# Dilated attention layer: TensorE order pinned, attention steps placed between dense products

## The chip, the cores and the metric

The kernel runs on one core of a Trainium2 chip. The metric is the time of one execution on the device in microseconds (us), the median of several runs.

## The reference

Two transformer blocks over 256 tokens of width 1024, fp32. The first has four layers, each an attention mixer and a SwiGLU FFN: differential attention (A), latent attention (B), dilated attention (C) and A again. The second block has two layers of a mixer with three branches and a convolutional FFN. The change lies in layer C, the third of the first block:

```python
C_GROUPS = ((128, 1), (512, 4), (2048, 16))   # window, dilation
C_HEADS = 16
C_HEAD_DIM = 64
...
    qkv = (h @ w_qkv).reshape(B, S, G, 3, C_HEADS, C_HEAD_DIM)
    q = apply_rope(qkv[:, :, :, 0], cos, sin) * (C_HEAD_DIM ** -0.5)
    k = apply_rope(qkv[:, :, :, 1], cos, sin)
    v = qkv[:, :, :, 2]
...
    wts = jax.nn.softmax(jnp.stack(lses, axis=0), axis=0)
    o = jnp.sum(wts[..., None].astype(v.dtype) * jnp.stack(outs, axis=0), axis=0)
    return o.reshape(B, S, C_HEADS * C_HEAD_DIM) @ w_o
```

Here `h` is the RMS-normalised input. Each of three groups looks at keys of its window and dilation; the groups are weighted by the softmax of their log-sums, so that one softmax over the scores of all three groups gives the same. Then come the residual and the FFN.

## The kernel before

All activations lie transposed in SBUF, 128 features by 256 tokens, eight such pieces for `x`. A dense product in fp32 is made of three matmuls (`mm3`, L259 to L261): both factors are split into a high and a low part, and high x high, high x low and low x high are added in PSUM. Weights come in tiles of 128x1024 by a DMA on the SyncE queue (`weights`, L271, tile `raw`, ring of `RAW` = 6); ScalarE writes the high part `whi` (through the helper `act`, L229) and VectorE the low part `wlo` (L276), both in rings of `SPL` = 6.

PSUM has three banks for dense products (`mm`), three for scores (`sc`) and two for transposes (`tp`).

Layer C (`dilated`) works in four quads of heads. For a quad, `qk_block` makes q and k of each of the three groups: `mmode` runs 48 products of 512 columns (two token halves, t = 0 and 1, in one `mm` bank each), ScalarE evicts them as `qtok` with the norm's factor `r`, VectorE rotates them, and they are transposed. For groups 1 and 2 four transposes per token half go into one `tp` bank, which ScalarE and VectorE copy out (`kz`, L613, the keys of two heads beside zeros). The first group needs more exact scores: `stacked` splits q and k again and transposes three groups of four (L570 q, L574 high k, L579 low k), each group into a `tp` bank that ScalarE (q, low k) or VectorE (high k, L575) empties. For every other quad `v_block` makes v for two quads in the same way.

The attention of a quad is eight steps (c, e, t: pair of heads, head, token half). A step is the scores (L860 for groups 1 and 2, L585 and L586 for the stacked ones, one `sc` bank), masking with the minimum on VectorE (L398, `aexp`), the exponential on ScalarE with its sum, reciprocal and normalising on VectorE (L869, L870), four transposes (L287) and their copy `aT` on VectorE (L875). After four steps 32 small products mix v (L882) into a `tp` bank, which is split into the output's pieces (`split`, L405). At the end `project` multiplies by w_co, 192 products of 256 columns, and adds to x (L888). The FFN follows with `rms`: squares on ScalarE, their sum on POOL (L438, `sqacc`), a matmul over ones (L444), power on POOL (L453).

The code is written quad after quad. A scheduler decides the order of the instructions on each engine before the kernel runs, by its own estimate of when each can start: it puts steps of one quad between dense products of the next as their inputs come ready.

Of the kernel before, what the change touches and what calls it, by code (L numbers as in the profile page):

```python
# [2 lines left out]

# [23 lines left out]
RAW, SPL, PIECES = 6, 6, 2  # L27
# [178 lines left out]
class Program:  # L206
    def __init__(self, tc, ins, out, at):
        self.tc, self.nc, self.ins, self.out, self.at = tc, tc.nc, ins, out, at
        self.ready = []
        with ExitStack() as ctx:  # L210
# [35 lines left out]
    def t2(self, name, shape=(512,)):  # L246
        return self.wk.tile([128, *shape], F32, name=name, tag="t2", bufs=7)
# [6 lines left out]

    def mm3(self, out, l, r, start, stop, **kw):
        lh, ll = l
        rh, rl = r
        mm = self.nc.tensor.matmul
# [27 lines left out]
    def transpose(self, out, in_):  # L286
        return self.nc.tensor.transpose(out, in_, self.ident)  # L287
# [21 lines left out]
    def mmode(self, aps, n, kb, xs):  # L309
        ps = [self.mm_bank()[:, :n] for _ in range(2)]  # L310
        for b, ap in enumerate(aps):
# [4 lines left out]
            for k, t in kt:  # L316
# [4 lines left out]
                         b == 0 and k == 0, b == len(aps) - 1 and k == kb - 1)  # L321
        return ps
# [118 lines left out]
    def rstd(self, acc, n, eps):  # L441
        ps = self.tp_bank()
        for t in range(2):
            self.nc.tensor.matmul(ps[:, t:t + 1], acc[:, t * 128:(t + 1) * 128], self.ones[:, 0:1],  # L444
                                  start=True, stop=True)
# [105 lines left out]
    def stacked(self, q, out, t):  # L551
# [17 lines left out]
        for h in range(4):  # L569
            nc.tensor.transpose(pt[:, h, :], sv[:, h, :], self.identr)  # L570
        a = self.act(qs[:, :, tk], pt)
        pt = self.tp_bank().bitcast(R).rearrange("p (c n) -> p c n", c=4)
        for h in range(4):
            nc.tensor.transpose(pt[:, h, :], k[:, h].rearrange("p a d -> p (a d)"), self.identr)  # L574
# [3 lines left out]
        for h in range(4):  # L578
            nc.tensor.transpose(pt[:, h, :], lo[:, h].rearrange("p a d -> p (a d)"), self.identr)  # L579
        self.act(kl[:, :, tk], pt)  # L580

    def stacked_scores(self, ps, qk, h, tk, start=True):

        qs, kd, kl = qk
        self.nc.tensor.matmul(ps, qs[:, h, tk], kd[:, h, :], start=start, stop=False)  # L585
        return self.nc.tensor.matmul(ps, qs[:, h, tk], kl[:, h, :], start=False, stop=True)  # L586

    def qk_block(self, w, xs, rms, tab, kz=None, scale=0.125):


        ps = self.mmode([w[0], w[1]], 512, 4, xs)
        r = rms()
# [3 lines left out]
        r8 = rms.r8  # L596
        stacked = kz is None
        out = [self.rslot(), self.rslot(), self.rslot()] if stacked else self.slot()[:, :2, :]
        for t in range(2):
            q = self.t2("qtok")  # L600
            self.act(q[:, :256], ps[t][:, :256], scale=r8[:, t:t + 1])
# [3 lines left out]
            if stacked:  # L605
                self.stacked(q, out, t)
                continue
            pt = self.tp_bank().rearrange("p (c n) -> p c n", c=4)
            for c in range(4):
                self.transpose(pt[:, c, :], q[:, c * 128:(c + 1) * 128])  # L610
            tk = slice(t * 128, t * 128 + 128)
            self.act(kz[0:64, 0, :, tk], pt[0:64, 2:4, :])
            self.nc.vector.tensor_copy(kz[64:128, 1, :, tk], pt[64:128, 2:4, :])  # L613
            self.act(out[:, :, tk], pt[:, 0:2, :])
        return out if stacked else (out, kz)
# [213 lines left out]
    def dilated(self, l, own):  # L829
# [18 lines left out]
        for hq in range(4):  # L848

            qk = [self.qk_block(wqk[g, hq], xs, r, "ropeC", kz[hq % 2][g], -0.125) for g in range(3)]  # L850
            if hq % 2 == 0:
                v = [self.v_block([wv[g, hq], wv[g, hq + 1]], xs, r) for g in range(3)]
            for c in range(2):
                es = {}
                for e in range(2):
                    for t in range(2):
                        tk = slice(t * 128, t * 128 + 128)
                        ps = self.sc_bank()
                        for g in (1, 2):
                            nc.tensor.matmul(ps[:, 128 * g + 128:128 * g + 256], qk[g][0][:, c, tk],  # L860
                                             qk[g][1][:, e, c, tk], start=True, stop=True)
                        self.stacked_scores(ps[:, :256], qk[0], 2 * c + e, tk)
                        mx = self.wk.tile([128, 1], F32, name="cmax", bufs=3)
                        ex = self.t2("aexp")
                        self.masked(ex, ps, self.maskC[:, t * 512:(t + 1) * 512], mx)
                        sm = self.wk.tile([128, 1], F32, name="csum", bufs=3)
                        self.act(ex, ex, AF.Exp, scale=-1.0, bias=mx, accum=sm)
                        rc = self.wk.tile([128, 1], F32, name="crec", bufs=3)
                        nc.vector.reciprocal(rc, sm)  # L869
                        nc.vector.tensor_scalar(ex, ex, rc, None, op0=OP.mult)  # L870
                        pt = self.tp_bank().rearrange("p (c n) -> p c n", c=4)
                        for kc in range(4):
                            self.transpose(pt[:, kc, :], ex[:, kc * 128:(kc + 1) * 128])
                        es[e, t] = self.t2("aT", (4, 128))
                        nc.vector.tensor_copy(es[e, t], pt)  # L875
# [601 lines left out]
```

## Time and profile before

| | us |
|---|---|
| median of 3 runs | 2367.68 (2367.56 to 2369.26) |
| the profiled execution | 2368.34 |
| its span | 2366.6 |
| PE busy | 2238.3 (95%) |
| VectorE (DVE) busy | 1699.8 (72%) |
| ScalarE (ACT) busy | 1297.7 (55%) |
| POOL busy | 425.3 (18%) |
| mean granted PE clock | 0.973 |

The span is the profiled execution's time between its first and its last instruction. PE, the matmul engine, bounds it; an instruction of another engine matters where PE waits for its result. The clock is the share of full speed (2.4 GHz) that PE was granted; at 0.50 (1.2 GHz) a matmul takes twice as long. Layer C reaches from 634.5 to 974.8 us.

### The profile page before, as it was taken

What the parts mean: (1) busy time and instruction counts of PE and PEld (TensorE: products, weight loads), DVE (VectorE), ACT (ScalarE), POOL (GpSimd) and SP (SyncE); (2) the same over time, 40 slices, a digit from 0 to 9 for tenths busy, and PEclk for the clock granted to TensorE, in tenths of its full rate; (3) what the DMA queues carried; (4) which work ended last, traced back from release to release, by engine and by line L of the source; (5) the groups of instructions that cost most, each with busy time, mean ns of one, the idle gap of its engine ahead of it and who ended that gap; (6) DMA issues with size and microseconds to landing.
All of it is one profiled execution on the core that took longest, in us unless ns stands there. A gap on an engine that the chain in (4) does not pass through costs nothing. (4 is left out here: it accounts for less than half of the span.)

```text
span 2366.6 us, 42382 instructions
## 1 busy us (share of the span) xinstructions
PE 2238.3 (95%) x16438; PEld 2087.9 (88%) x16438; DVE 1699.8 (72%) x2984; ACT 1297.7 (55%) x2352; POOL 425.3 (18%) x345
## 2 busy tenths in 40 slices
PE   8999999999998898899999999988989999798998
PEld 6899997999977787899988999877989998698998
DVE  6776656766556656766677767896798689858875
ACT  7764465544554444544587545543457564345763
POOL 1010012200100000100102002264352034434211
PEclk9999999999999999999999999998989999898999
DMA  6355553455653243355633656433435554243543
GB/s 241 125 165 184 157 161 107 142 185 157 196 181 104 97 160 99 131 186 156 210 126 108 217 158 196 148 123 102 157 131 194 162 178 156 98 135 133 188 155 104
DMA packets 111417, 361.76 MB, mean 153 GB/s; under 512 B 12400, under 2 KB 15600, under 8 KB 111216
## 3 DMA queue, kind: packets, MB, share of 16 engines
q1 hardware_dynamic: 108816, 355.45, 45.9%
q10 hardware_dynamic: 2256, 3.34, 0.4%
q8 instruction: 129, 2.11, 0.4%
q14 instruction: 72, 0.59, 0.1%
q0 software_dynamic: 144, 0.26, 0.1%
HBM read 358.22 MB, written 1.05 MB: 152 GB/s over the span
## 5 line engine op out<-in xcount | busy, mean ns | idle before, releaser
L229 ACT ACTIVATE whi<-raw 128x1024 fp32r<-128x1024 f32 (+2 forms) x744 | 722.2, 976 | 588.6 <-PE mm L260 295.0
L276 DVE TENSOR_TENSOR wlo<-raw,whi 128x1024 fp32r<-128x1024 f32 (+4 forms) x686 | 774.2, 1133 | 320.2 <-ACT whi L229 319.1
L259 PE MATMUL mm<-xh,whi 128*128 128x256 f32 x2496 | 712.7, 286 | 6.0 <-DVE early L1124 5.8
L260 PE MATMUL mm<-xl,whi 128*128 128x256 f32 x2496 | 712.0, 285 | 4.5 <-DVE xl L232 4.3
L261 PE MATMUL mm<-xh,wlo 128*128 128x256 f32 x2496 | 711.2, 285 | 2.6 <-DVE wlo L276 2.6
L259 PEld LDWEIGHTS mm<-xh,whi 128*128 128x128 f32 x2496 | 479.4, 192 | 8.8 <-issue 7.0
L260 PEld LDWEIGHTS mm<-xl,whi 128*128 128x128 f32 x2496 | 479.1, 192 | 6.9 <-DVE xl L232 5.7
L261 PEld LDWEIGHTS mm<-xh,wlo 128*128 128x128 f32 x2496 | 478.5, 192 | 4.0 <-DVE wlo L276 3.2
L259 PE MATMUL mm<-s,whi 128*128 128x256 f32 x1504 | 428.1, 286 | 7.4 <-DVE s L232 5.1
L260 PE MATMUL mm<-s,whi 128*128 128x256 f32 x1504 | 426.1, 284 | 0.0
L261 PE MATMUL mm<-s,wlo 128*128 128x256 f32 x1504 | 425.6, 284 | 0.0
L259 PEld LDWEIGHTS mm<-s,whi 128*128 128x128 f32 x1504 | 287.5, 192 | 12.7 <-DVE s L232 4.6
L260 PEld LDWEIGHTS mm<-s,whi 128*128 128x128 f32 x1504 | 288.1, 192 | 1.2 <-issue 0.8
L261 PEld LDWEIGHTS mm<-s,wlo 128*128 128x128 f32 x1504 | 288.2, 192 | 0.1
L259 PE MATMUL mm<-whi,xh 128*128 128x512 f32 (+3 forms) x608 | 240.0, 396 | 10.4 <-ACT whi L229 8.6
L260 PE MATMUL mm<-wlo,xh 128*128 128x512 f32 (+3 forms) x608 | 238.7, 393 | 0.9 <-DVE wlo L276 0.8
L261 PE MATMUL mm<-whi,xl 128*128 128x512 f32 (+3 forms) x608 | 238.0, 392 | 0.0
L276 POOL TENSOR_TENSOR wlo<-raw,whi 128x1024 fp32r<-128x1024 f32 x58 | 142.2, 2461 | 150.6 <-ACT whi L229 150.3
L438 POOL TENSOR_TENSOR sqacc<-sqacc,sq 128x256 f32<-128x256 f32 x56 | 59.5, 1063 | 584.0 <-ACT sq L229 581.3
L259 PEld LDWEIGHTS mm<-whi,xh 128*128 128x128 f32 x608 | 115.1, 189 | 32.7 <-ACT whi L229 8.6
L260 PEld LDWEIGHTS mm<-wlo,xh 128*128 128x128 f32 x608 | 115.2, 190 | 21.4 <-DVE wlo L276 2.0
L261 PEld LDWEIGHTS mm<-whi,xl 128*128 128x128 f32 x608 | 115.1, 189 | 20.5
(328 smaller groups left out, 2863.6 us busy)
## 6 DMA issues: line engine op xcount, KB each, us to landing
raw<-w_gu SPq DMA_DIRECT2D x176, 512.0 KB, 4.5
raw<-w_up SPq DMA_DIRECT2D x88, 512.0 KB, 4.2
raw<-w_zs SPq DMA_DIRECT2D x60, 512.0 KB, 3.9
raw<-w_out SPq DMA_DIRECT2D x64, 384.0 KB, 3.1
raw<-w_cqk SPq DMA_DIRECT2D x48, 512.0 KB, 4.3
raw<-w_out SPq DMA_DIRECT2D x64, 320.0 KB, 3.1
raw<-w_aqk SPq DMA_DIRECT2D x32, 512.0 KB, 4.4
raw<-w_cv SPq DMA_DIRECT2D x24, 512.0 KB, 3.9
```

The source lines that it names most:

```text
L229: return self.nc.scalar.activation(out, in_, func, bias=bias, scale=scale, **kw)
L259: mm(out, lh, rh, start=start, stop=False, **kw)
L260: mm(out, lh, rl, start=False, stop=False, **kw)
L261: return mm(out, ll, rh, start=False, stop=stop, **kw)
L276: e.tensor_sub(lo, raw, hi.bitcast(F32))
L438: self.nc.gpsimd.tensor_add(acc, acc, sq)
```

## The change

In layer C every matmul and transpose on PE is kept in the order in which the code issues it (`keep_in_program_order`), and the code issues it in a new order. `mmode` counts modelled time after each `mm3` (`tick`), and a queue (`later`) calls steps when their modelled time has come; `drain` empties the queue, up to a condition, without dense products.

- v of a quad pair comes before q and k, and a quad's groups in the order 1, 2, 0.
- The transposes of q and k, the scores, the turn (transposes of the exponentials) and the mixing products are steps in that queue, each with a delay behind what feeds it: 4.2 and 5.8 for the two token halves of groups 1 and 2, 5.5 and 7.9 for the stacked ones, 4.5 from scores to turn, 2.2 from turn to mixing.
- Mixing is done for each token half apart (16 products, into an `sc` bank); the splits of its result become 16 of half the size.
- The copy `aT` moves from VectorE to ScalarE (32).
- The eight steps of the last quad are issued between 132 of the 192 output products; the other 60 are not pinned. The additions to x follow each pair of pieces, and the last pair uses an `sc` bank.
- `RAW` is 5 and not 6; the ring `t2` (qtok, aexp, aT) has 9 buffers and not 7.

The number of matmuls stays the same. Of the diff, the functions that decide the order (in `qk_block` the part behind the product became a generator, `qk_tokens`; the body of `score` is that of before):

```diff
-RAW, SPL, PIECES = 6, 6, 2
+RAW, SPL, PIECES = 5, 6, 2
+US = {128: 0.11, 256: 0.12, 512: 0.235}
...
-        return self.wk.tile([128, *shape], F32, name=name, tag="t2", bufs=7)
+        return self.wk.tile([128, *shape], F32, name=name, tag="t2", bufs=9)
...
+    def matmul(self, *a, **kw):
+        i = self.nc.tensor.matmul(*a, **kw)
+        if self.woven:
+            self.tc.keep_in_program_order(i)
+        return i
+
+    def later(self, delay, step):
+        self.serial += 1
+        heappush(self.queue, (self.now + delay, self.serial, step))
+
+    def tick(self, us):
+        self.now += us
+        if not self.inside:
+            self.inside = True
+            while self.queue and self.queue[0][0] <= self.now:
+                heappop(self.queue)[2]()
+            self.inside = False
+
+    def drain(self, done=lambda: False):
+        while self.queue and not done():
+            self.now = max(self.now, self.queue[0][0])
+            self.tick(0.0)
...
-    def transpose(self, out, in_):
-        return self.nc.tensor.transpose(out, in_, self.ident)
+    def transpose(self, out, in_, ident=None):
+        i = self.nc.tensor.transpose(out, in_, self.ident if ident is None else ident)
+        if self.woven:
+            self.tc.keep_in_program_order(i)
+        return i
...
                 self.mm3(ps[t], (xh[:, tk], xl[:, tk]), w(k, 0, n),
                          b == 0 and k == 0, b == len(aps) - 1 and k == kb - 1)
+                if self.woven:
+                    self.tick(3 * US[n])
...
+        self.woven = True
+        v, done = {}, [0]
+        def values(hq):
+            for g in range(3):
+                v[hq // 2, g] = self.v_block([wv[g, hq], wv[g, hq + 1]], xs, r)
+        def queries(hq):
+            q12 = self.slot()
+            qk = {}
+            for g in (1, 2, 0):
+                ps = self.mmode([wqk[g, hq][0], wqk[g, hq][1]], 512, 4, xs)
+                toks = list(self.qk_tokens(ps, r, "ropeC", -0.125))
+                if g:
+                    qk[g] = q12[:, 2 * g - 2:2 * g, :], kz[hq % 2][g]
+                    for t in range(2):
+                        self.later(4.2 + 1.6 * t, lambda t=t, q=toks[t], o=qk[g]: feature(q, o, t))
+                else:
+                    qk[0] = [self.rslot(), self.rslot(), self.rslot()]
+                    for t in range(2):
+                        self.later(5.5 + 2.4 * t, lambda t=t, q=toks[t]: (self.stacked(q, qk[0], t), self.tick(0.9)))
+            return qk
+        def feature(q, out, t):
+            qT, kT = out
+            tk = slice(t * 128, t * 128 + 128)
+            pt = self.tp_bank().rearrange("p (c n) -> p c n", c=4)
+            for c in range(4):
+                self.transpose(pt[:, c, :], q[:, c * 128:(c + 1) * 128])
+            self.act(kT[0:64, 0, :, tk], pt[0:64, 2:4, :])
+            nc.vector.tensor_copy(kT[64:128, 1, :, tk], pt[64:128, 2:4, :])
+            self.act(qT[:, :, tk], pt[:, 0:2, :])
+            self.tick(0.44)
+        def score(hq, qk, c, t, e, es):
+            tk = slice(t * 128, t * 128 + 128)
...
+            self.tick(0.7)
+            self.later(4.5, lambda: turn(hq, c, t, e, ex, es))
+        def turn(hq, c, t, e, ex, es):
+            pt = self.tp_bank().rearrange("p (c n) -> p c n", c=4)
+            for kc in range(4):
+                self.transpose(pt[:, kc, :], ex[:, kc * 128:(kc + 1) * 128])
+            es[e] = self.t2("aT", (4, 128))
+            self.act(es[e], pt)
+            self.tick(0.44)
+            if e:
+                self.later(2.2, lambda: mix(hq, c, t, es))
+        def mix(hq, c, t, es):
+            if (hq // 2, 2) not in v:
+                return self.later(1.0, lambda: mix(hq, c, t, es))
+            po = self.sc_bank()[:, :128]
+            for kc in range(4):
+                g, tv = (0, kc) if kc < 2 else (kc - 1, t)
+                for e in range(2):
+                    h = hq % 2 * 256 + (2 * c + e) * 64
+                    self.matmul(po[64 * e:64 * e + 64, :], v[hq // 2, g][:, tv, h:h + 64],
+                                es[e][:, kc, :], start=kc == 0, stop=kc == 3)
+            oh, ol = os_[hq * 2 + c]
+            tk = slice(t * 128, t * 128 + 128)
+            self.split(oh[:, tk], ol[:, tk], po, 1.0)
+            done[0] += 1
+            self.tick(1.3)
+        def attention(hq, qk, delay, pace):
             for c in range(2):
                 for t in range(2):
+                    es = {}
+                    for e in range(2):
+                        self.later(delay, lambda c=c, t=t, e=e, es=es: score(hq, qk, c, t, e, es))
+                        delay += pace
+        values(0)
+        qk = queries(0)
+        attention(0, qk, 11.0, 5.4)
+        qk = queries(1)
+        attention(1, qk, 11.0, 5.0)
+        qk = queries(2)
+        self.drain(lambda: done[0] == 8)
+        attention(2, qk, 26.0, 5.4)
+        values(2)
+        qk = queries(3)
+        self.drain(lambda: done[0] == 12)
+        attention(3, qk, 10.5, 1.9)
+        last = lambda j, k, f: self.mm3(ps[j][:, f, :], wt[j](k, f * 128), os_[k], k == 0 and f == 0,
+                                        k == 7 and f == 1, skip_group_check=True)
+        ps, wt = {}, {}
+        for j in range(4):
+            wt[j] = self.weights(self.ins["w_co"][j], 256)
+            ps[j] = (self.mm_bank() if j < 3 else self.sc_bank()).rearrange("p (f n) -> p f n", f=2)
+            for k in range(6 if j < 3 else 4):
+                for f in range(2):
+                    last(j, k, f)
+                    self.tick(3 * US[256])
+        self.drain()
+        self.woven = False
+        for j in range(4):
+            for k in range(6 if j < 3 else 4, 8):
+                for f in range(2):
+                    last(j, k, f)
+            for f in range(2):
+                k = 2 * j + f
+                xv = perm(self.x[k])
+                nc.vector.tensor_add(xv, xv, flat(ps[j][:, f, :]))
```

How this moves instructions is shown at three places. The first is PE at the start of layer C: `sqacc` is the sum of squares, `mm_7739` and `mm_7740` (before), `mm_7671` and `mm_7672` (after) are banks of the product blocks being started. Before:

```order
L444 MATMUL tp_7661<-ones_80,sqacc_7638 128x1 [waits Pool_49]
...
L259 MATMUL mm_7739<-whi_7743,xh_76 128x512 [waits Activation_49]
L260 MATMUL mm_7739<-wlo_7744,xh_76 128x512 [waits DVE_49]
L261 MATMUL mm_7739<-whi_7743,xl_77 128x512
...
L261 MATMUL mm_7739<-whi_7779,xl_77 128x512
L259 MATMUL mm_7740<-whi_7743,xh_76 128x512 [waits PE_49,Activation_49]
```

After:

```order
L261 MATMUL tp_7662<-ones_80,sqacc_7639 128x1 [waits Pool_49]
...
L261 MATMUL mm_7671<-whi_7675,xh_76 128x512 [waits Activation_49]
L261 MATMUL mm_7671<-wlo_7676,xh_76 128x512 [waits DVE_49]
L261 MATMUL mm_7671<-whi_7675,xl_77 128x512
L261 MATMUL mm_7672<-whi_7675,xh_76 128x512 [waits Activation_49]
```

Before, fifteen products for one token half stand behind the matmul over ones ahead of the first for the other half; after, three do, and the fourth waits for ScalarE.

The second is PE at the stacked transposes of a quad (`qsplit`, `ksplit`, `klow` are the split parts of q and k). Before, both token halves:

```order
L570 MATMUL tp_8474<-identr_78,qsplit_8467 128x128 [waits DVE_49,PE_49]
L574 MATMUL tp_8480<-identr_78,ksplit_8468 128x128 [waits PE_49,Activation_49]
L260 MATMUL mm_8526<-wlo_8536,xh_76 128x512
...
L579 MATMUL tp_8486<-identr_78,klow_8469 128x128 [waits DVE_49,Activation_49]
L570 MATMUL tp_8507<-identr_78,qsplit_8500 128x128 [waits DVE_49]
L260 MATMUL mm_8526<-wlo_8566,xh_76 128x512
...
L574 MATMUL tp_8513<-identr_78,ksplit_8501 128x128 [waits Activation_49]
L579 MATMUL tp_8519<-identr_78,klow_8502 128x128 [waits DVE_49,Activation_49]
```

After, one token half (the first of each four transposes is shown, here and above):

```order
L261 MATMUL mm_8677<-whi_8686,xl_77 128x512
L315 MATMUL tp_8728<-identr_78,qsplit_8721 128x128 [waits DVE_49,PE_49]
L315 MATMUL tp_8734<-identr_78,ksplit_8722 128x128 [waits Activation_49]
L315 MATMUL tp_8740<-identr_78,klow_8723 128x128 [waits DVE_49,Activation_49]
L261 MATMUL mm_8676<-whi_8748,xh_76 128x512
```

Before, dense products lie between eight, eight and eight; after, each half's twelve follow one another.

The third is PE at the end of the last quad (`pk0` is the identity, `aexp` the exponentials, `mm_10416` and `mm_10204` output products). Before:

```order
L261 MATMUL mm_10416<-s4_7561,wlo_10413 128x256
L287 MATMUL tp_10232<-pk0_70,aexp_10225 128x128 [waits DVE_49,PE_49]
L287 MATMUL tp_10232<-pk0_70,aexp_10225 128x128 x3
L287 MATMUL tp_10252<-pk0_70,aexp_10245 128x128 [waits DVE_49,PE_49]
L287 MATMUL tp_10252<-pk0_70,aexp_10245 128x128 x3
L882 MATMUL tp_10259<-aT_10197,s4_9368 64x128 [waits PE_49]
```

After, one step of several:

```order
L261 MATMUL mm_10204<-s4_7561,wlo_10201 128x256
L315 MATMUL tp_10274<-pk0_70,aexp_10214 128x128 [waits DVE_49,PE_49]
L315 MATMUL tp_10274<-pk0_70,aexp_10214 128x128 x3
L261 MATMUL sc_10281<-kz10_7527,s4_9587 128x128 [waits PE_49]
...
L261 MATMUL mm_10204<-s4_7561,whi_10200 128x256
...
L315 MATMUL tp_10300<-pk0_70,aexp_10236 128x128 [waits DVE_49]
L315 MATMUL tp_10300<-pk0_70,aexp_10236 128x128 x3
```

Before, the last two turns follow one another with the mixing products behind them; after, a turn, the scores of a later step and six output products alternate.

## Rows read from the trace of the kernel before

**Rows 1.** The page: busy time per engine; granted PE clock in 40 slices (tenths).

```profile
PE 2238.3 (95%) x16438; PEld 2087.9 (88%) x16438; DVE 1699.8 (72%) x2984; ACT 1297.7 (55%) x2352; POOL 425.3 (18%) x345
...
PEclk9999999999999999999999999998989999898999
```

**Rows 2.** Waits of PE, 634.5 to 981.3: us in total, times, longest.

```profile
PE tp L287 <- DVE aexp L870: 23.5, 8, 3.1
PE tp L287 <- DVE qtok L390: 2.2, 8, 0.4
...
PE mm L259 <- ACT qtok L229: 0.9, 1, 0.9
...
PE mm L259 <- ACT s L229: 0.5, 1, 0.5
```

**Rows 3.** Timeline of PE, end of the first quad: start, us, instruction, idle before.

```profile
740.67 1.09 PE L287 MATMUL tp<-pk,aexp 128*128 128x128 f32 x4 [2.87 <-DVE aexp L870]
744.86 1.09 PE L287 MATMUL tp<-pk,aexp 128*128 128x128 f32 x4 [3.11 <-DVE aexp L870]
```

**Rows 4.** Timeline of DVE, the step whose transposes start at 740.67.

```profile
738.21 0.68 DVE L398 CUSTOM_DVE_ANT_0 aexp<-sc,maskC 128x512 f32<-128x512 f32 x1
...
740.04 0.48 DVE L870 TENSOR_SCALAR aexp<-aexp,crec 128x512 f32<-128x512 f32 x1
```

**Rows 5.** Stretches: length, busy us of PE, PEld, DVE, ACT, POOL, clock, DMA.

```profile
634.50:974.80 340.30, 311.93 (x1799) 255.71 (x1798) 211.40 (x404) 173.24 (x303) 13.95 (x13) 0.95 0.37 123
...
740.18:750.42 10.24, 6.64 (x42) 5.54 (x43) 5.18 (x17) 3.66 (x10) 0.00 (x0) 0.50 0.01 2
805.04:811.87 6.83, 5.20 (x37) 4.50 (x38) 3.18 (x12) 3.26 (x9) 0.00 (x0) 0.50 0.00 0
897.20:907.44 10.24, 6.68 (x42) 5.54 (x43) 5.18 (x17) 3.70 (x10) 0.00 (x0) 0.50 0.00 0
958.64:965.47 6.83, 4.13 (x34) 3.83 (x36) 2.27 (x6) 0.81 (x2) 0.98 (x2) 0.50 0.01 2
371.54:378.37 6.83, 5.69 (x20) 5.39 (x21) 2.35 (x7) 3.26 (x7) 1.54 (x1) 0.50 0.31 101
```

**Rows 6.** Groups by form, 634.5 to 974.8: busy us, mean ns, idle before.

```profile
L276 DVE TENSOR_TENSOR wlo<-raw,whi 128x1024 fp32r<-128x1024 f32 x80 | 100.1, 1255 | 61.9 <-ACT whi L229 61.5
L229 ACT ACTIVATE whi<-raw 128x1024 fp32r<-128x1024 f32 x81 | 85.2, 1057 | 53.1 <-PE mm L261 30.7 <-issue 16.8 <-ACT qtok L229 2.4
...
L875 DVE COPY aT<-tp 128x512 f32<-128x512 f32 x32 | 22.1, 690 | 25.0 <-PE tp L287 25.0
...
L229 ACT ACTIVATE s<-tp 128x512 fp32r<-128x512 f32 x16 | 9.0, 583 | 0.8 <-PE tp L579 0.6
...
L229 ACT ACTIVATE s<-mm,rstd 128x512 f32<-128x512 f32 x12 | 8.3, 688 | 12.0 <-PE mm L261 12.0
```

**Rows 7.** Timelines of PE and POOL at the start of the layer.

```profile
647.56 0.39 PE L260 MATMUL mm<-wlo,xh 128*128 128x512 f32 x1
647.80 0.39 PE L261 MATMUL mm<-whi,xl 128*128 128x512 f32 x1
...
649.10 1.63 POOL L453 TENSOR_TENSOR rstd<-ms,nhalf 128x2 f32<-128x2 f32 x1 [2.37 <-DVE ms L451]
```

**Rows 8.** Timeline of PE, a wait in the latent layer before.

```profile
372.68 0.63 PE L287 MATMUL tp<-pk,qtok 128*96 128x128 f32 x2 [3.06 <-DVE arec L808]
```

**Rows 9.** Timeline of PE, stacked transposes of the third quad.

```profile
813.57 0.51 PE L574 MATMUL tp<-identr,ksplit 128*128 128x128 f32 x4
813.91 0.46 PE L260 MATMUL mm<-wlo,xh 128*128 128x512 f32 x1
```

**Rows 10.** Timelines of POOL and PE behind the layer.

```profile
972.09 9.06 POOL L438 TENSOR_TENSOR sqacc<-sqacc,sq 128x256 f32<-128x256 f32 x7 [11.33 <-ACT sq L229]
...
981.32 0.50 PE L444 MATMUL tp<-ones,sqacc 128*128 128x1 f32 x4
```

**Rows 11.** The page: issues of DMA, KB each, us to landing.

```profile
raw<-w_cqk SPq DMA_DIRECT2D x48, 512.0 KB, 4.3
```

More of the change, by code (lines that the diff above doesn't have):

```diff
@@ L2 @@
 from contextlib import ExitStack
+from heapq import heappop, heappush
 import numpy as np
@@ L209, in __init__ @@
         self.ready = []
+        self.woven, self.now, self.queue, self.inside, self.serial = False, 0.0, [], False, 0
         with ExitStack() as ctx:
@@ L443, in rstd @@
         for t in range(2):
-            self.nc.tensor.matmul(ps[:, t:t + 1], acc[:, t * 128:(t + 1) * 128], self.ones[:, 0:1],
-                                  start=True, stop=True)
+            self.matmul(ps[:, t:t + 1], acc[:, t * 128:(t + 1) * 128], self.ones[:, 0:1],
+                        start=True, stop=True)
         return self.power(ps[:, 0:2], 1.0 / n, eps)
@@ L604, in qk_block @@
             self.rope(q.rearrange("p (h d) -> p h d", h=8)[:, :, :16], 8, 8, c2, s2)
[L605 to L615, printed above, removed]
+            yield q
     def v_block(self, w, xs, r):
@@ L847, in dilated @@
         os_ = self.split_slots(8)
[L848 to L852, printed above, removed]
-            for c in range(2):
[L854 to L875, printed above, removed]
-                po = self.tp_bank()[:, :256]
-                for t in range(2):
-                    for kc in range(4):
-                        g, tv = (0, kc) if kc < 2 else (kc - 1, t)
-                        for e in range(2):
-                            h = hq % 2 * 256 + (2 * c + e) * 64
-                            nc.tensor.matmul(po[64 * e:64 * e + 64, t * 128:t * 128 + 128], v[g][:, tv, h:h + 64],
-                                             es[e, t][:, kc, :], start=kc == 0, stop=kc == 3)
-                self.split(*os_[hq * 2 + c], po, 1.0)
@@ new lines, in feature @@
+        def feature(q, out, t):
[10 more added lines that the diff above has]
+            tk = slice(t * 128, t * 128 + 128)
+            ps = self.sc_bank()
+            for g in (1, 2):
+                self.matmul(ps[:, 128 * g + 128:128 * g + 256], qk[g][0][:, c, tk],
+                            qk[g][1][:, e, c, tk], start=True, stop=True)
+            self.stacked_scores(ps[:, :256], qk[0], 2 * c + e, tk)
+            mx = self.wk.tile([128, 1], F32, name="cmax", bufs=3)
+            ex = self.t2("aexp")
+            self.masked(ex, ps, self.maskC[:, t * 512:(t + 1) * 512], mx)
+            sm = self.wk.tile([128, 1], F32, name="csum", bufs=3)
+            self.act(ex, ex, AF.Exp, scale=-1.0, bias=mx, accum=sm)
+            rc = self.wk.tile([128, 1], F32, name="crec", bufs=3)
+            nc.vector.reciprocal(rc, sm)
+            nc.vector.tensor_scalar(ex, ex, rc, None, op0=OP.mult)
+            self.tick(0.7)
+            self.later(4.5, lambda: turn(hq, c, t, e, ex, es))
```

28 lines of the change are left out of this document (13 added, 15 removed).

## The prediction

> **What bounds the kernel now.** I read the page first. TensorE (PE) is busy for 95% of the span, so only its idle time and its slow stretches can be won; the strip of granted clock shows where it falls below full speed [rows 1]. The reader should see there that nothing general is wrong: a gain can only come out of particular holes. The waits of PE over the changed layer, from its first dense product at 634.5 to the first products of the FFN behind it, name those holes [rows 2]: eight waits for the normalised exponentials (`aexp`, DVE L870), 23.5 us in all, the longest 3.1, then eight short ones for the rotated q and k (2.2 us), and one at the start of the layer (0.9).
>
> The timeline says where the eight lie. The first quad of heads runs its eight attention steps between dense products of the next quad; its last two steps find no products left, and PE stands before their transposes for 2.87 and 3.11 us [rows 3]. The other three quads end alike, the last two waits of the eight being 2.43 and 3.11. The wait is a chain of one step: masking on DVE starts at 738.21, the transposes can start 2.46 us later, when DVE has normalised [rows 3, 4]. So 24 of 32 steps are covered by products and 8 are not.
>
> The table of stretches adds what the holes cost behind them [rows 5]. After each of the four ends the granted clock is 0.50, 1.2 instead of 2.4 GHz, for 10.24, 6.83, 10.24 and 6.83 us. PE was busy in these for 6.64 + 5.20 + 6.68 + 4.13 = 22.65 us, work of half that time at full clock: 11.3 us lost. **The four ends cost 23.5 + 0.5 + 11.3 = 35.3 us**, with 0.5 for the output products' wait for the last split [rows 2].
>
> **What the change removes.** Every matmul of the layer is pinned, and a queue counts modelled time (0.235 us for a 512-column product; 0.24 on the timeline [rows 7]) and puts scores, transposes and mixing products between dense ones, the steps of the last quad between output products. The dense products, scores, transposes and mixing products stay the same in number. So the four ends go, if the placing works: -35.3. The feature transposes are put 4.2 and 5.8 modelled us behind their product block, so the 2.2 us of waits for q and k go too [rows 2]. Floor: 2368.3 - 35.3 - 2.2 = 2330.8.
>
> **What it adds,** part by part.
>
> *Start of the layer.* Today the scheduler runs 15 products of one token half into the third bank while the norm is being computed, and then waits 0.9 us [rows 2]. Pinned, token halves alternate after every three products, and the fourth needs a bank that ScalarE (ACT) must first empty. The three end at about 648.2 (the third starts at 647.80, lasts 0.39). The emptying needs the power on POOL, done at 649.10 + 1.63 = 650.73 [rows 7], and one value eviction of 0.69 [rows 6]: 651.5 at the earliest. A wait of 3.4 in place of 0.9: +2.5. A wait of 3.06 earlier in the program [rows 8] lies beside a stretch of 6.83 us at clock 0.50 with 5.69 busy [rows 5], 2.85 lost; I take that as well: +2.9. Ends: 2 and 6. Sum here +5.4.
>
> *Stacked transposes* (q and split k of the first group, eight token halves). Today they come as eight, products, four or the like; two groups of four lie 0.34 us apart with no idle time [rows 9]. Now all twelve come in a row, on two PSUM banks, so the third four waits until the first bank is copied out: 0.46 us for the transposes, 0.58 for the copy on ACT [rows 6], less some 0.6 that PE needs to get there, leaves 0.4 to 0.5. When the ACT stands in a weight split (1.06 us, 81 of them in the layer, [rows 6]) it is up to 1.5. I take 0.8, nearer to the lower value since splits fill a quarter of ACT's time: 8 x 0.8 = +6.4; ends 0 and 10. The Trainium skill, "Perfetto Trace Analysis", section "Matmuls" (under "Optimizing Tensor Performance"), says that independent matmul groups should rotate through PSUM banks so that the emptying of one lies beside the next one's matmuls; twelve in a row on two banks go against it. By the rule this term exists, and by today's rows, which show no wait, it would be nothing and the sum 6.4 lower; the present order puts products between, so the trace agrees with the rule rather than with a zero.
>
> *Turns.* Each step's transposes come 4.5 modelled us after its score, in the traced costs 3.8 to 5.1 us of PE work, for a chain of 2.46 [rows 3, 4]. A weight split on each engine can stand ahead of a link: 1.06 on ACT, 1.26 on DVE [rows 6], 4.8 together, which a short cover misses by up to 1. Only some steps meet both: +2 over the steady steps; ends 0 and 6. The copy of transposed weights moves from DVE to ACT (32 x 0.69, [rows 6]): DVE falls from 211 us of the 340, ACT rises from 173 to 195, both far from full [rows 5]. No added cost of its own beyond the turns.
>
> *Two drains.* Where the queue is emptied between quads, the last transposes are followed at once by the mixing products that wait for the ACT copy: 0.69 and a semaphore, +1 (0 to 2). Among the output products the last steps lie beside products and beside each other's scores and mixing, with short holes behind the last copy and split: +1. At worst the last two waits come back whole, 6.
>
> *Start of the FFN.* Today POOL adds squares from 972.09 for 9.06 us (seven, 1.29 each) and the matmul over ones, behind the FFN's first 48 products, comes at 981.32, just after, without waiting [rows 10]. In the new order 36 output products stand between the end of the second x pair and the FFN, 24 behind the third; at 0.12 us the third pair is ready 2.9 us before it. ACT squares the second pair only behind the high parts of the third, some 2.5 us later, so six additions begin about 0.4 us before the FFN and end -0.4 + 6 x 1.29 = 7.3 us into it, while the matmul over ones is due behind 48 products of 0.12, after 5.7. +1.7, with the semaphores (0 to 4).
>
> *Ring of raw weights 6 to 5.* A 512 KB transfer takes 4.3 us to land [rows 11]; with both splits (1.06 + 1.26) a buffer is bound for 6.6 us, a fifth of it 1.3, and PE needs 12 x 0.235 = 2.8 us per tile. Nothing; hidden by dense work. Outside the layer the order changes by a few places in one attention layer and the convolutional FFN: 0, bounds -3 and +3.
>
> **The sum:** 2330.8 + 5.4 + 6.4 + 2 + 1 + 1 + 1.7 = 2348.3 against the profiled execution of 2368.3. The median of the runs, 2367.7, is 0.7 lower, so 2347.6; I say **2348**, -0.8%. A measurement of this kernel can tell about 0.2%, 4.7 us, from no change.
>
> **Rivals.**
>
> 1. *New waits all hidden* (start and FFN too, at their low ends): the floor plus 2 to 5, about **2334**. For it: 24 of today's steps run without a wait. Against: the bank limit at the start is forced by order. Chance 0.15.
>
> 2. *Slower: the pinned order waits at every turn.* PE may not run ahead any more; when `aexp` is late, dense products that are ready stand behind the transposes. The price is the mean wait per turn times 32. It cancels the gain at (2368.3 - 2346.3) / 32 = 0.7 us; a mean of 1.0, from a cover at 3.8 against a chain of 4.8 at every step, gives 2346.3 + 32 = **2378**, and more if the clock falls with it. For it: the copy now also sits on ACT ahead of the next exponential (0.69). Against: splits take 85 us of ACT and 100 of DVE in 340 [rows 5, 6], a quarter, so most links meet none. Chance 0.08.
>
> 3. *The last quad's end stays* because output products run out too early: 2.43 + 3.11 + 0.5 and half of 4.13 [rows 5] come back, 8.1, **2356**. Against: 132 products are woven in. Chance 0.06.
>
> 4. *Weights late* through the smaller ring, in bursts behind the reordered transfers: some 10 us, **2358**. Against: the arithmetic above. Chance 0.05.
>
> 5. *The change does nothing*, because the scheduler had reached the same order: **2367**. Against: the two orders differ at the places shown. Chance 0.03.
>
> **How the numbers follow.** The forecast has 0.61 and, by its terms' ends, reaches from 2330 to 2368; the other 0.02 is for causes that I don't see, slower. A range of **2336 to 2362** leaves out most of the first rival, the second and fifth, and the forecast's rim: about 2 in 10. Faster: forecast, rivals 1, 3 and 4 = 0.87; same: rival 5 and a little of 2 = 0.04; slower 0.09.
>
> **What would show it.** In the profile after, PE's waits for `aexp` should be under 6 us and none over 1.5, with no stretch at clock 0.50 in the four places; one wait of some 3.4 us after three products at the layer's start, with a low clock beside it; eight waits of 0.4 to 1.5 on the third four of the stacked transposes; a wait of 1 to 4 at the matmul over ones. The forecast is wrong if waits for `aexp` come back as 32 of about 1 us (rival 2), if whole waits of 2.5 to 3 us stand before the output products' end (3), or if waits for weight splits appear between dense products (4).

## The result and the profile after

The changed kernel takes 2340.99 us (median of 4 runs, 2339.84 to 2341.94), the one before 2367.99: ratio 0.9885, 95% interval 0.9868 to 0.9902. The forecast was 2348 in a range of 2336 to 2362; the gain came out at 27 us where 20 were forecast. The profiled execution of the changed kernel took 2339.84 us.

The page after, as in [rows 1]:

```profile
PE 2223.0 (95%) x16438; PEld 2078.4 (89%) x16438; DVE 1677.6 (72%) x2960; ACT 1316.7 (56%) x2392; POOL 422.4 (18%) x345
...
PEclk9999999999999999999999999988999999899999
```

PE is busy for 15 us less with the same number of instructions, mostly because fewer of them run at half clock: 100.6 us of its busy time lay in stretches at 0.50 before, 72.3 do now, and half of the difference is 14.2. Where the time went is best read between two points that both kernels have: the matmul over ones for the norm at the start of layer C, and that for the FFN behind it. Before, they start at 646.78 and 981.32 [rows 10], 334.54 us apart:

```profile
646.78 0.61 PE L444 MATMUL tp<-ones,sqacc 128*128 128x1 f32 x4 [0.96 <-POOL sqacc L438]
```

After, at 645.93 and 955.40, 309.47 apart: **25.1 of the 28.5 us of span lie in the layer.** (Below, "the layer" is this distance.) The waits of PE in it, to be read beside [rows 2]:

```profile
PE tp L315 <- ACT s L232: 4.6, 8, 1.0
PE mm L261 <- ACT s L232: 3.3, 1, 3.3
PE sc L261 <- ACT aT L232: 2.0, 1, 2.0
PE mm L261 <- ACT qtok L232: 1.1, 1, 1.1
PE mm L261 <- DVE xl L235: 1.0, 1, 1.0
PE tp L261 <- POOL sqacc L471: 1.0, 1, 1.0
PE tp L315 <- DVE s L608: 0.8, 1, 0.8
```

All products now have one line, L261, and all transposes L315. The reader should see that no wait for `aexp` and none for rotated q and k is left (23.5 and 2.2 us before), and that seven groups are listed now, 13.8 us in all. Two of these were there before: the wait at the matmul over ones (1.0), and that for the low part of x (`xl`, 1.0 now), which has this row in the list of before:

```profile
PE mm L260 <- DVE xl L232: 0.6, 1, 0.6
```

Of the four stretches at clock 0.50 none is left, and there is a new one at 648.44:

```profile
633.60:948.40 314.80, 301.66 (x1800) 251.01 (x1799) 190.43 (x377) 191.04 (x341) 12.44 (x11) 0.99 0.41 136
...
648.44:655.27 6.83, 4.62 (x11) 3.65 (x12) 1.02 (x2) 1.64 (x3) 1.44 (x1) 0.50 0.77 266
```

It lies beside the new wait at the start of the layer, seen on the timelines of PE, ACT and POOL:

```profile
645.93 0.61 PE L261 MATMUL tp<-ones,sqacc 128*128 128x1 f32 x4 [0.97 <-POOL sqacc L471]
...
646.95 0.40 PE L261 MATMUL mm<-whi,xl 128*128 128x512 f32 x1
650.65 0.80 PE L261 MATMUL mm<-whi,xh 128*128 128x512 f32 x1 [3.31 <-ACT s L232]
...
649.91 1.27 ACT L232 ACTIVATE s<-mm,rstd 128x512 f32<-128x512 f32 x2 [3.27 <-POOL rstd L486]
...
648.25 1.63 POOL L486 TENSOR_TENSOR rstd<-ms,nhalf 128x2 f32<-128x2 f32 x1 [2.37 <-DVE ms L484]
```

Three products, then PE waits 3.31 us for the first value eviction, which waits for the power on POOL. The stacked transposes show the other forecast wait, here one of the two longest of the eight (0.99 and 1.00), with ACT beside it:

```profile
715.46 0.50 PE L315 MATMUL tp<-identr,ksplit 128*128 128x128 f32 x4
716.96 0.54 PE L315 MATMUL tp<-identr,klow 128*128 128x128 f32 x4 [0.99 <-ACT s L232]
...
715.36 1.06 ACT L232 ACTIVATE whi<-raw 128x1024 fp32r<-128x1024 f32 x1 [1.20 <-PE mm L261]
716.33 0.58 ACT L232 ACTIVATE s<-tp 128x512 fp32r<-128x512 f32 x1
```

The low parts of k need the bank of q; its copy stands behind a weight split of 1.06 on ACT and starts only at 716.33. Where the queue is drained, the same happens to the copy of transposed exponentials:

```profile
819.85 0.88 PE L261 MATMUL sc<-aT,s 128*64 128x128 f32 x12 [2.05 <-ACT aT L232]
...
818.26 1.05 ACT L232 ACTIVATE whi<-raw 128x1024 fp32r<-128x1024 f32 x1
819.21 0.59 ACT L232 ACTIVATE aT<-tp 128x512 f32<-128x512 f32 x1
```

At the end of the last quad, where PE waited 2.43 and 3.11 us before, transposes and mixing products follow without a wait:

```profile
936.92 0.60 PE L315 MATMUL tp<-pk,aexp 128*128 128x128 f32 x4
...
937.80 1.09 PE L261 MATMUL sc<-aT,s 128*64 128x128 f32 x16
938.83 0.66 PE L315 MATMUL tp<-pk,aexp 128*128 128x128 f32 x4
```

(The trace counts each fp32 mixing product twice: the sixteen of a token half, here and in the text on the change, are eight instructions.) And at the start of the FFN:

```profile
948.28 0.28 PE L261 MATMUL mm<-xh,whi 128*128 128x256 f32 x1
948.55 6.68 POOL L471 TENSOR_TENSOR sqacc<-sqacc,sq 128x256 f32<-128x256 f32 x6 [2.17 <-ACT sq L232]
...
953.84 0.39 PE L261 MATMUL mm<-xl,whi 128*128 128x256 f32 x1 [1.00 <-DVE xl L235]
...
955.40 0.50 PE L261 MATMUL tp<-ones,sqacc 128*128 128x1 f32 x4
```

POOL ends its squares at 955.23, just ahead of the matmul over ones, which doesn't wait. The wait of 1.00 is another: VectorE is late with the low part of x.

### The profile page after: what moved, and what is told of

It reads as the page before. It is cut to its first block, busy times and chain, and to the rows that moved or that the text cites. A ratio compares the mean times of both kernels' runs of the same rounds, so it can differ in the third digit from the quotient of the medians.

```text
span 2338.1 us, 42371 instructions
## 1 busy us (share of the span) xinstructions
PE 2223.0 (95%) x16438; PEld 2078.4 (89%) x16438; DVE 1677.6 (72%) x2960; ACT 1316.7 (56%) x2392; POOL 422.4 (18%) x345
## 3 DMA queue, kind: packets, MB, share of 16 engines
HBM read 358.22 MB, written 1.05 MB: 154 GB/s over the span
## 5 line engine op out<-in xcount | busy, mean ns | idle before, releaser
L261 PE MATMUL mm<-xl,whi 128*128 128x256 f32 x2496 | 711.0, 285 | 4.9 <-DVE xl L235 4.7
L261 PE MATMUL mm<-xh,whi 128*128 128x256 f32 x2496 | 712.5, 286 | 2.0 <-DVE early L1232 1.9
L261 PE MATMUL mm<-xh,wlo 128*128 128x256 f32 x2496 | 710.1, 285 | 2.6 <-DVE wlo L304 2.6
L261 PE MATMUL mm<-s,whi 128*128 128x256 f32 x2976 | 545.6, 285 | 6.8 <-DVE s L235 6.5
L261 PEld LDWEIGHTS mm<-xl,whi 128*128 128x128 f32 x2496 | 478.3, 192 | 7.2 <-DVE xl L235 6.1
L261 PEld LDWEIGHTS mm<-xh,whi 128*128 128x128 f32 x2496 | 478.9, 192 | 5.2 <-DVE early L1232 2.3
L261 PEld LDWEIGHTS mm<-xh,wlo 128*128 128x128 f32 x2496 | 477.7, 191 | 3.7 <-DVE wlo L304 3.2
L261 PEld LDWEIGHTS mm<-s,whi 128*128 128x128 f32 x2976 | 465.2, 192 | 13.3 <-DVE s L235 4.6
L261 PE MATMUL mm<-s,wlo 128*128 128x256 f32 x1488 | 421.1, 283 | 0.0
L261 PEld LDWEIGHTS mm<-s,wlo 128*128 128x128 f32 x1488 | 285.1, 192 | 0.1
L261 PE MATMUL mm<-whi,xh 128*128 128x512 f32 (+3 forms) x608 | 242.4, 400 | 13.4 <-ACT whi L232 8.7
L261 PE MATMUL mm<-wlo,xh 128*128 128x512 f32 (+3 forms) x608 | 238.1, 392 | 0.9 <-DVE wlo L304 0.8
L261 PE MATMUL mm<-whi,xl 128*128 128x512 f32 (+3 forms) x608 | 237.5, 391 | 0.0
L261 PEld LDWEIGHTS mm<-whi,xh 128*128 128x128 f32 x608 | 115.2, 190 | 35.4 <-ACT whi L232 8.7
L261 PEld LDWEIGHTS mm<-whi,xl 128*128 128x128 f32 x608 | 115.3, 190 | 22.6
L261 PEld LDWEIGHTS mm<-wlo,xh 128*128 128x128 f32 x608 | 115.5, 190 | 21.2 <-DVE wlo L304 2.0
L232 ACT ACTIVATE s<-guh 128x256 fp32r<-128x256 f32 x132 | 54.9, 416 | 120.0 <-DVE guh L523 94.4
L235 DVE SCALAR_TENSOR_TENSOR cv<-cvp,pk,cv 128x256 f32<-128x256 f32 x120 | 92.5, 809 | 0.4
```

Of the source, the lines that this page charges most:

```text
L232: return self.nc.scalar.activation(out, in_, func, bias=bias, scale=scale, **kw)
L235: return self.nc.vector.scalar_tensor_tensor(out, a, s, b, op0=op0, op1=op1)
L261: i = self.nc.tensor.matmul(*a, **kw)
```

## The experiments

Three theories stood against each other. **Theory 1, placing:** the code's order, which puts each step where products cover its chain, removes the four ends; each new wait costs what its row shows. **Theory 2, pinning:** holding the scheduler to that order is what does it. **Theory 3, rings:** the larger t2 ring or the smaller raw ring does part of it. Single runs of one kernel spread over up to 13 us here, so each run is judged by its layer, from its own trace; the median and the ratio to the kernel before, run beside it (its median was 2368 to 2370 us), stand behind. "Layer" comes from the two matmuls over ones on each trace's PE timeline (the same number of dense products lies between them in every run), the waits are the sum of the list of PE's waits between them, the clock column the length of the stretches at 0.50. Each layer is from one execution; the changed kernel, traced twice, gave 309.47 and 309.81.

| run | layer us | waits of PE in it | clock 0.50, us | median us | ratio (95%) |
|---|---|---|---|---|---|
| before | 334.54 | 28.7 | 34.1 | 2367.99 | |
| after | 309.47 | 13.8 | 6.8 | 2340.99 | 0.9885 (0.9868 to 0.9902) |
| e12 (after, again) | 309.81 | 13.8 | 6.8 | 2341.72 | 0.9888 (0.9874 to 0.9902) |
| e1 unpinned | 299.32 | 3.8 | 3.4 | 2333.47 | 0.9846 (0.9832 to 0.9859) |
| e2 old rings | 309.35 | 13.9 | 6.8 | 2343.57 | 0.9890 (0.9874 to 0.9906) |
| e3 before, new rings | 333.17 | 29.3 | 27.3 | 2368.07 | 0.9988 (0.9978 to 0.9998) |
| e4 copy on DVE | 310.32 | 15.8 | 6.8 | 2343.48 | 0.9884 (0.9867 to 0.9901) |
| e5 start | 305.53 | 10.6 | 3.4 | 2339.31 | 0.9876 (0.9861 to 0.9891) |
| e6 stacked apart | 307.74 | 11.4 | 10.2 | 2342.75 | 0.9889 (0.9874 to 0.9904) |
| e7 no drain | 307.44 | 11.7 | 6.8 | 2338.66 | 0.9864 (0.9847 to 0.9882) |
| e8 e5 to e7 together | 297.74 | 5.0 | 0 | 2329.70 | 0.9833 (0.9818 to 0.9848) |
| e9 short cover | 326.12 | 26.1 | 10.2 | 2357.84 | 0.9958 (0.9945 to 0.9972) |
| e10 last quad apart | 331.69 | 28.2 | 23.9 | 2366.74 | 0.9990 (0.9979 to 1.0001) |
| e11 best | 294.02 | 2.0 | 0 | 2327.28 | 0.9820 (0.9801 to 0.9838) |

### e1: nothing pinned

```diff
         i = self.nc.tensor.matmul(*a, **kw)
-        if self.woven:
-            self.tc.keep_in_program_order(i)
         return i
```

(and the same in `transpose`).

> The changed kernel, its queue and its order in the code kept, but nothing pinned on TensorE: the scheduler may move each matmul. Theory 1 (placing): the gain comes from where the code puts the steps, so the four ends stay away; the scheduler splits most of the twelve stacked transposes and saves some of their 5 us of waits: 2335 to 2341 us, waits for aexp under 2 us. Theory 2 (pinning): the scheduler bunches steps as before once it is free, and waits of 2.4 to 3.1 us with a low clock come back at the quads' ends: 2355 to 2368 us.

The layer takes 299.32 us, ten less than pinned, and PE's waits in it are three:

```profile
PE mm L261 <- ACT s L232: 1.9, 1, 1.9
PE mm L261 <- DVE xl L235: 1.0, 1, 1.0
PE tp L261 <- POOL sqacc L467: 0.9, 1, 0.9
```

No wait for `aexp`: theory 2 falls. The order in the code is enough; the scheduler keeps the steps nearly where the code puts them. (The old order with a pin was not run.) The pin costs ten microseconds of the layer: with it PE stands at the eight stacked transposes, at the drain and at a bank for `qtok`, where the free order puts a few products between, and at the start for 3.3 us instead of 1.9. At the first stacked transposes, where the pinned kernel waits 0.99, there are now four products between these two rows:

```profile
718.79 0.51 PE L313 MATMUL tp<-identr,ksplit 128*128 128x128 f32 x4
...
720.29 0.54 PE L313 MATMUL tp<-identr,klow 128*128 128x128 f32 x4
```

The median, 2333.47 us, is below even theory 1's range of 2335 to 2341, which counted only on part of the stacked waits.

### e2 and e3: the rings

e2 is the changed kernel with the old rings, e3 the kernel before with the new ones.

```diff
-RAW, SPL, PIECES = 5, 6, 2
+RAW, SPL, PIECES = 6, 6, 2
...
-        return self.wk.tile([128, *shape], F32, name=name, tag="t2", bufs=9)
+        return self.wk.tile([128, *shape], F32, name=name, tag="t2", bufs=7)
```

> The changed kernel with the rings of before: 6 raw buffers, 7 in t2. Theory 1: outside the layer the 3.4 us that were won come back, and inside it the steps, which hold qtok, aexp and aT longer, wait a little for buffers: 2343 to 2349 us. Theory 3 (the rings make the gain in the layer): the pinned order runs out of t2 buffers at most steps, 1 us each or so: 2360 to 2380 us.

> The kernel before with only the rings changed: 5 raw buffers, 9 in t2. Theory 1: layer C keeps its four ends, outside it about 3.4 us are won: 2363 to 2366 us. Theory 3: with more t2 buffers the scheduler runs ahead and the ends shrink: under 2358 us.

With old rings the layer is the same to 0.1 us. Put into the kernel before, the new ones leave its first row of waits as it was:

```profile
PE tp L287 <- DVE aexp L870: 23.5, 8, 3.1
```

So theory 3 falls, and with it the part of theory 1 that put a 3.4 us gain outside the layer down to the rings: e3's ratio is a gain of 0.02 to 0.22%, its layer is 1.4 us shorter, as two of the stretches at half clock came out at 6.83 instead of 10.24 us (17.1 instead of 22.6 us of busy PE at half clock, 2.8 saved) while PE's waits grew by 0.6, and behind the layer its trace is no shorter than before (1385.8 us against 1385.2 from the second matmul over ones to the end of the span).

### e4: the copy back on VectorE

```diff
-            self.act(es[e], pt)
+            nc.vector.tensor_copy(es[e], pt)
```

> The changed kernel with the copy of the transposed exponentials back on VectorE. Theory 1: ScalarE and VectorE both have room (191 and 190 of 315 us busy in the layer), so the copy's place matters only at the drain, where ScalarE is waited for: 2339 to 2343 us. Rival: the copy stands ahead of weight splits on VectorE, which are on the path of the dense products, or turns are late: over 2345 us.

310.32 us, 0.9 more; the wait at the drain is the same on the other engine, and POOL's squares come later:

```profile
PE tp L261 <- POOL sqacc L471: 2.4, 2, 1.4
...
PE sc L261 <- DVE aT L934: 2.0, 1, 2.0
```

(1.4 of the 2.4 stands at the start of the FFN, the other 1.0 at that of the layer.) Both engines have the room; where the copy stands hardly matters.

### e5, e6, e7: the new waits one by one

e5 takes the second v block's first token half whole before the second half:

```diff
+        if halves:
+            ws = [self.weights(ap, n) for ap in aps]
+            for t in range(2):
+                tk = slice(t * 128, t * 128 + 128)
+                for kk in range(2 * kb):
+                    xh, xl = xs[kk]
+                    self.mm3(ps[t], (xh[:, tk], xl[:, tk]), ws[kk // kb](kk % kb, 0, n), kk == 0, kk == 2 * kb - 1)
+                    self.tick(3 * US[n])
+            return ps
...
+                v[hq // 2, g] = self.v_block([wv[g, hq], wv[g, hq + 1]], xs, r, hq == 0 and g == 1)
```

> The changed kernel, but the second v block of the layer takes all 24 products of the first token half before those of the second. Theory 1: the wait of 3.31 us after three products goes, and with it the 6.83 us at half clock beside it (4.62 busy, 2.3 lost); in return up to 1 us of waiting for weights that are needed twice as fast: 2335 to 2338 us. Rival (the wait only moves to the weights): 2340 to 2342 us.

e6 puts the four low transposes later:

```diff
+        def low():
...
+            self.act(kl[:, :, tk], pt)
+        if self.woven:
+            self.tick(0.9)
+            self.later(1.1, low)
```

> The changed kernel, with the last four of each half's twelve stacked transposes put six dense products later. Theory 1: the eight waits before them (0.34 to 1.00 us, 5.0 in all) go: 2335 to 2337 us. Rival (the same copy is waited for at the next bank user): 2340 to 2342 us.

e7 brings the second quad's steps closer:

```diff
-        attention(1, qk, 11.0, 5.0)
+        attention(1, qk, 11.0, 4.5)
```

> The changed kernel with the second quad's steps 4.5 instead of 5.0 modelled us apart, so that its last transposes and mixing products lie between dense products instead of following each other where the queue is drained. Theory 1: the wait of 2.05 us goes: 2338 to 2340 us. Rival (shorter distances make turns late elsewhere): 2341 us or more, with waits for aexp.

In their layers: e5 saves 3.9 us. The wait of 3.31 and the low clock beside it are gone, worth 5.6 together, and no wait for weights came; 1.7 came back in this execution, in 3.41 us of busy PE at half clock behind the drain. e6 saves only 1.7, and its rival is partly right: the waits fall from 4.6 + 0.8 to 2.9 us, as partly another bank user now waits (the next half's high k, up to 1.00), and this execution has the 3.41 us at half clock, too.

```profile
PE tp L315 <- ACT s L232: 2.9, 5, 1.0
PE sc L261 <- ACT aT L232: 2.2, 2, 2.0
```

e7 saves 2.0, the whole wait at the drain (mixing waits once, for 0.2, at another step):

```profile
PE tp L315 <- ACT s L232: 5.3, 8, 1.0
...
PE sc L261 <- ACT aT L232: 0.2, 1, 0.2
```

In the medians these three can't be told from the changed kernel, whose interval theirs overlap; e5 (2339.31) and e6 (2342.75) lie above the ranges that theory 1 gave them, e7 (2338.66) inside. What tells them apart is the lists of waits, which agree to 0.1 us in the two traces of the changed kernel. The stretches at half clock come or stay away after equal waits (last section), so the savings of 1.7 to 3.9 us, from one trace each, are rough.

### e8: the three together

> The changed kernel with the three edits together: first token half first in the second block, the low transposes put later, the second quad's steps closer. Theory 1: the three savings lie at different places and add up: 2328 to 2333 us. Rival (one hides another): 2335 us or more.

297.74 us in the layer, 11.7 less than the changed kernel, where the three alone add to 7.7: none hides another, and the half-clock stretches, of which each single run kept one or two, are gone as well. 2329.70 us, ratio 0.9833.

### e9: a cover that is too short

```diff
-            self.later(4.5, lambda: turn(hq, c, t, e, ex, es))
+            self.later(2.5, lambda: turn(hq, c, t, e, ex, es))
```

> The changed kernel with the turn 2.5 instead of 4.5 modelled us behind its score: mostly 12 products, 2.8 us, lie between, against a chain of 2.46 without any weight split in it. This is the slower rival of the prediction, made. Theory 1: a split of 1.06 on ScalarE or 1.26 on VectorE in the chain is then waited for, 0.3 to 1.0 us at most of the 24 turns between dense products, 7 to 24 us over the layer's 309: 2348 to 2365 us. Rival (the splits fall beside the chain, or the clock drops with every wait): within 3 us of 2341, or above 2370.

The slower rival's mechanism, with less cover:

```profile
PE tp L315 <- DVE aexp L925: 13.9, 15, 2.3
PE tp L315 <- ACT s L232: 4.6, 10, 1.0
```

15 turns wait for `aexp`, 0.9 us on average; the layer grows by 16.7 us, the median by 16.9, inside the 7 to 24 expected. Between the end of a step's scores and the place of its turn PE now has 2.4 to 4.0 us, in the changed kernel 3.8 to 6.3. The longest wait has a weight split of each engine in its chain, ahead of the exponential (ACT) and of the normalising (DVE):

```profile
788.42 1.06 ACT L232 ACTIVATE whi<-raw 128x1024 fp32r<-128x1024 f32 x1 [1.14 <-PE mm L261]
...
789.51 1.23 DVE L304 TENSOR_TENSOR wlo<-raw,whi 128x1024 fp32r<-128x1024 f32 x1 [0.29 <-ACT whi L232]
...
791.39 0.66 PE L315 MATMUL tp<-pk,aexp 128*128 128x128 f32 x4 [2.31 <-DVE aexp L925]
```

The scores of that step end at 786.3, so its chain took 5.1 us. The mechanism is real, and 4.5 modelled us avoided it at all 32 turns; distances between 2.5 and 4.5 were not run.

### e10: the last quad apart

```diff
-        attention(3, qk, 10.5, 1.9)
+        attention(3, qk, 10.5, 5.4)
+        self.drain()
```

> The changed kernel with the last quad's eight steps ahead of all output products, one after another, instead of between them. Theory 1: now all eight turns of that quad are uncovered, up to 2.5 us each less the two that overlap, and the clock halves beside them: 15 to 30 us more, 2356 to 2371 us. Rival (the products behind the layer only start earlier and the FFN waits as long): within 3 us of 2341.

```profile
PE tp L315 <- DVE aexp L925: 10.1, 5, 2.5
...
PE tp L315 <- DVE qsplit L596: 3.8, 2, 2.4
...
PE sc L261 <- ACT aT L232: 2.9, 4, 2.0
```

The drain also leaves this quad's stacked transposes without products, hence the waits for `qsplit`. The layer grows by 22.2 us, with one stretch of 17.07 us at half clock, and the kernel is as slow as the one before: 14.4 us more of waits, and 6.2 for the clock (half of 17.11 - 4.62 busy). One quad with none of its eight steps covered costs nearly as much as the change gains in all four, of which the old order left two steps each uncovered.

### e11: the best parts, and e12: the changed kernel again

e11 is e1 with the edits of e5 and e7.

> The best of the earlier runs put together: nothing pinned, first token half first in the second v block, second quad's steps 4.5 modelled us apart. Theory 1: of the waits in the layer only those at the norm (1.0) and at the start of the FFN (1.0) are left, and no low clock: the layer takes 295 to 297 us between the two norm matmuls, 309.5 in the changed kernel: 2326 to 2332 us. Rival (unpinned, the scheduler undoes the new start): the layer stays at 299 us, 2333 us.

> The changed kernel once more, beside the one before it: what its layer and its time are on this chip. Theory 1: layer at 309 to 310 us between the two norm matmuls, 2341 us within 0.15%.

e11's layer takes 294.02 us with two waits left:

```profile
PE mm L261 <- DVE xl L235: 1.0, 1, 1.0
PE tp L261 <- POOL sqacc L476: 1.0, 1, 1.0
```

No stretch at half clock lies in it. The median is 2327.28 us, the ratio 0.9820 (0.9801 to 0.9838), against 0.9888 (0.9874 to 0.9902) for the changed kernel on the same chip: the intervals don't meet, and it beats both kernels. The layer is 1 us under the 295 to 297 expected. From e8, pinned and with all three edits (0.9818 to 0.9848), the medians can't tell it.

## Why the prediction was right

**The floor.** The four ends (35.3 us) and the waits for q and k (2.2) went entirely, as forecast. e9 and e10 show that cover is what did it: made shorter, it costs 16.7 us, and taken from one quad 22.2, with everything else of the change in place. Whether other parts of it (mixing by token halves and in an `sc` bank, v first, the order of the groups) helped the layer was not run apart.

**The new waits** were forecast at 17.5 us, measured 13.6 in the trace:

| term | forecast | measured |
|---|---|---|
| start of the layer: wait | +2.5 | 3.31 - 0.89 = +2.4 |
| start: clock | +2.9 | half of 4.62 = +2.3 |
| eight stacked transposes | +6.4 | 4.6 + 0.8 - 0.3 = +5.1 |
| turns between products | +2 | +0.3 |
| drain | +1 | +2.0 |
| last quad | +1 | 0 |
| start of the FFN | +1.7 | 1.0 - 0.6 = +0.4 |
| a bank for `qtok` | none | +1.1 |

(0.3 of the 4.6 is the one turn that waits, for a transpose bank that ACT empties.) 2.4 + 2.3 + 5.1 + 0.3 + 2.0 + 0.4 + 1.1 = 13.6, and 37.5 - 13.6 = 23.9 of the layer's 25.1. The remaining 1.2 has no row of its own. Against the profiled execution the forecast (2348.3) was 8.5 us too high: 3.9 in these terms, that 1.2, and 3.4 outside the layer.

**The terms that were mis-sized.** In the layer it is most of all "*Turns* ... +2 over the steady steps", which took a split ahead of a link as likely; none of the 32 turns waited for `aexp`. e9 shows that a chain with both splits is as long as the forecast had it (5.1 us, 4.8 forecast); in the changed kernel no such chain met a cover too short for it, and why the splits fell better there stays open. "*Two drains*" was too small, since a weight split of 1.05 stood ahead of the copy on ACT. The wait of 1.1 for a bank that `qtok` holds was missed. At the start of the layer the forecast's own rows give 651.42 - 648.19 = 3.2 where it wrote 3.4; 3.31 came.

"*Start of the FFN*" was off by 1.3 us, and what came is not its mechanism. It forecast a wait of 1 to 4 us at the matmul over ones, for POOL's squares, and there is none. The squares' start was nearly right (948.55, 0.3 us behind the first FFN product at 948.28 instead of 0.4 ahead), but the six additions took 6.68, 1.11 each, not 1.29. (The row of before, 9.06 for seven, holds only 0.5 of gaps; the additions themselves were longer there, and why is open.) And the wait of 1.00 for the low part of x, which is what the table has, put the matmul over ones off to 955.40, behind the end of the squares; without it some 0.8 us would have been waited there, as an estimate from these times. In e4 and e9 the forecast's wait did come, 1.39 and 1.38. The waits at the start of the layer, at the stacked transposes and at the drain came at the places and for the reasons forecast.

**Rule and trace.** The wait at the stacked transposes, for which the prediction cited the Trainium skill ("Perfetto Trace Analysis", "Matmuls": rotate through banks), came as that rule has it: 5.1 us at eight places, none where e1 lets products come between.

**The rivals.** 1 (all hidden) gave about 2334: the measured 2341 lies as far from it as from the forecast of 2348, so the time alone does not decide between them. The waits do: it was nearer for the turns, and wrong for the start (3.31 us and the low clock) and the stacked transposes (5.1). 2 (waits at every turn) did not come, but e9 shows its price: 13.9 us of waits, still 8 us under the layer before. 3 (the last end stays) fell: nothing waits there. e10 is no price for it, since it uncovers all eight steps and not the last two. 4 (late weights) fell: no wait of PE in the changed kernel's layer names a weight split, and e2 with a sixth raw buffer has the same layer. 5 (nothing happens) fell.

**What the forecast did not ask** is whether the pin helps. It doesn't with this order: e1 without it has the better layer by ten microseconds. Most of this can be had with the pin as well, by edits to the order (e8, 297.74).

**Outside the layer** the forecast had 0, with bounds of 3 either way, and the two profiled executions differ by 3.4 us: 0.85 up to the first matmul over ones, 2.6 behind the second (1385.2 against 1382.7). That is the largest single miss. e12 repeats the second (1382.4), but the other runs made from the changed kernel lie between 1383.2 (e9) and 1387.0 (e11), on both sides of the 1385.2 of the kernel before and the 1385.8 of e3. So the 2.6 us are not shown to come from the change; what makes them stays open.

## What to carry to other kernels

A chain of small steps between engines is free only while enough independent products are placed after its start: count the chain and one long instruction on each engine it passes (here 2.46 us bare, 5.1 with a split on each), and look first at the ends of loops, where the products run out. The written order can give the scheduler the right places without pinning; a pin also takes away its freedom to slip a few products into every other short wait. Judge a change of one stage by that stage's length in the trace when single runs spread by more than it is worth.

## What the runs showed of the hardware

I had not expected that the clock of PE after a wait is not fixed by the length of that wait. The drain's wait of 2.04 or 2.05 us is followed by a stretch of 3.41 us at clock 0.50 in e5 (from 816.35) and e6 (from 819.73), and by none in the changed kernel, e10 and e12. The start's wait of 3.31 us has 6.83 us at clock 0.50 beside it in the changed kernel and 3.41 in e10. The longest stretch, 17.07 us, came in e10, in which waits of 0.2 to 2.5 us alternate with a few transposes and scores; eight waits of 0.34 to 1.00 us between dense products had no such stretch beside them in the changed kernel.
